# Gates and branch projections with tokens stationary, and another order of pooling, keys and branches, in a two-layer hybrid encoder

## Chip, core and metric

The kernel runs on one core of a Trainium2 chip. A time is the device time of one execution in microseconds (us). The engines are PE (matmul; PEld is its weight load), DVE (VectorE), ACT (ScalarE), POOL (GpSimd) and SP (which issues the weight DMAs).

## What is computed

Two layers of an encoder over 256 tokens of width 1024, all in float32. In each layer three mixers work on one normalised input, each is projected back to 1024, and the three are added under sigmoid gates; then follow an output projection and a gated MLP.

```python
def reference(...):
    for i in range(DEPTH):                                  # 2 layers
        h = _rms_norm(x, norm_mix_pre[i])                   # x: 256 tokens x 1024
        proj = h @ w_in[i]
        u_hy, q, k, v, g_out, gate_lr, u_pool, gate_logits = _split(proj, IN_SPLITS)
        y_hy = _hyena_mixer(u_hy, ...)                      # FFT long convolution, 512 wide
        y_gla = _gla_mixer(q, k, v, g_out, gate_lr, ...)    # gated linear attention, 4 heads
        y_pool = _pool_mixer(u_pool, ...)                   # 4 centred window means less input, 128 x 128 products
        gates = jax.nn.sigmoid(gate_logits).reshape(B, L, N_BRANCHES, D_MODEL)
        merged = (gates[:, :, 0] * (y_hy @ w_br_hyena[i])
                  + gates[:, :, 1] * (y_gla @ w_br_gla[i])
                  + gates[:, :, 2] * (y_pool @ w_br_pool[i]))
        x = x + _rms_norm(merged @ w_out[i], norm_mix_post[i])
        h = _rms_norm(x, norm_ffn_pre[i])
        a, b = _split(h @ ffn_w_up[i], (D_FF, D_FF))        # 2 x 2816
        a = _dwconv3_centred(a, ffn_conv_w[i], ffn_conv_b[i])
        y = (jax.nn.gelu(a, approximate=False) * b) @ ffn_w_down[i]
        x = x + _rms_norm(y, norm_ffn_post[i])
```

## The kernel before

**Matmuls.** Every float32 operand of a large product is split into a high part (ACT copies it with rounding to the matmul's format, L98 through `split` and `split_upper`) and a low part (DVE subtracts, L103), and a product is three matmuls: high by high, high by low, low by high. All matmuls go through `mm` (L112). The normalised input is kept transposed, channels on partitions and 256 tokens along the row (`xt`, four tiles of high and four of low parts in two halves).

**Weights** come in 71 chunks per layer of 128 x 2048 numbers (1 MB), in the order of `order`, by SP into three `raw` buffers (`dma_next`); a chunk's buffer is free when its low half is split off, and then the next chunk is fetched. A split chunk holds four of 37 `big` slots. `unit` writes down one piece of matmul work, forces the splits that it needs, writes down the pending work on its result (`post`), and steps the side work (`tick`: hyena, decay gates, pooling, linear attention), which is written as generators that wait for free slots.

**Two forms of matmul.** With weights stationary (`ftile`, `two_ftiles`) a 128 x 128 block of weights is loaded and 256 tokens stream past it: a chunk is 48 matmuls of 256 columns, and the result lies with channels on partitions. With tokens stationary (`chunk_x_stationary`) a 128 x 128 block of tokens is loaded and 512 columns of weights stream past: a chunk is 24 matmuls of 512 columns, and the result has tokens on partitions. The values, the output projection and the MLP's down projection use the second form; keys, queries, the inputs of hyena and pooling, gates, branches and most of the up projection use the first.

**Order of a layer.** Values and output gate, low-rank decay, hyena inputs, queries, keys (`qk_post(enb, ...)`), pooling inputs (`pool_post`, which starts `pool_pair`: window sums on DVE, then two small products), and then `branch` for hyena, pooling and linear attention: for each half of 512 channels two gate chunks, then one chunk of the branch projection, gate times projection on DVE, and for the later branches the sum. After the third branch the sum is split at once into the operands of the output projection, since it already has channels on partitions. `hyena()` transforms its input, multiplies the spectra on DVE (`p`, `q`, `p2`, `q2`), then asks for the inverse matrices (`ih`, `il`, two DMAs on POOL's queue, L804 and L805), and multiplies by them; its result is the operand of the first branch.

A scheduler sets the final order of instructions on each engine from this text. Around each layer's norms an explicit window keeps the written order. On each engine instructions run in the order that stands in the program.

Of the kernel before, what the change touches and what calls it, by code (L numbers as in the profile page):

```python
# [18 lines left out]
P = 128  # L19
# [11 lines left out]
NCHUNK = 71  # L31


V_HYC = 0
V_FFC = 48
V_GB = 136
V_PS = 148
V_FB = 152
NVEC = 160

UP_ORDER = (0, 4, 1, 5, 2, 6, 3, 7, 8, 9, 10)

# [34 lines left out]
def trunk(ctx: ExitStack, tc: tile.TileContext, a: dict, out: bass.AP):  # L77
# [87 lines left out]
    order = []  # L165
    for i in range(DEPTH):
        base = i * NCHUNK
        order += [("w", base + c) for c in range(4)]
        order.append(("lr", i))
        order += [("w", base + c) for c in range(4, NCHUNK)]  # L170
    pos_of = {o: n for n, o in enumerate(order)}
    raws, wh, wl = {}, {}, {}
    state = {"dma": 0, "h": 0, "l": 0}
# [1 line left out]
    def dma_next(parts=1, between=None):  # L175
        n = state["dma"]
        if n >= len(order):
            return
        kind, c = order[n]
        w = 2048 if kind == "w" else 512  # L180
        r = wpool.tile([P, w], F32, tag="raw", name=f"raw{n}")
        src = a["wts"][c] if kind == "w" else a["lrw"][c]
        for m in range(parts):
            s = slice(m * w // parts, (m + 1) * w // parts)
            nc.sync.dma_start(r[:, s], src[:, s])
            if between is not None and m == 0:
                between()
        raws[n] = r
        state["dma"] = n + 1
# [110 lines left out]
            n += 1  # L300
            assert n < 500, "side work cannot go on"

    pending = deque()
    prog = {"acc": 0.0}

    def unit(chunks, pe, post=None, cost=2.6, free=None):
        for c in chunks:
            while state["l"] < 2 * (c + 1):
                split_half()
        ahead["at"] = min(chunks)  # L310
        pe()
        if free is not None:
            big.put(*wh.pop(free), *wl.pop(free))
        while pending:
            pending.popleft()()
        if post is not None:
            pending.append(post)
        prog["acc"] += cost
        while prog["acc"] >= 2.6 - 1e-6:
            prog["acc"] -= 2.6  # L320
            tick()
            for _ in range(0 if ahead["still"] else 1 if ahead["quiet"] else 2):
                filler()

    def room(shape, dtype=F32):
        n = 0
        while not big.free:
# [239 lines left out]
    def layer(i, xt, chains):  # L567
        base = i * NCHUNK
        cur = {"c": 0}
        nxt = lambda: pos_of[("w", base + cur["c"])]  # L570

        def take():
            n = nxt()
            cur["c"] += 1
            return n
# [149 lines left out]
        def qk_post(dst, pair, scale):  # L725
            def post(ps):
                for z in range(2):
                    d = dst[pair][:, :, z, :]
                    if scale is None:
                        tt(d, ps[:], d, ALU.mult)  # L730
                    else:
                        stt(d, ps[:], scale, d)
            return post

        def hyena():
# [42 lines left out]
                    psm.put(ps)  # L778
            big.put(zth, ztl, even, kf.pop("dft"))
            yh, yl = [], []  # L780
            for b in range(2):
                while len(big.free) < 2:
                    yield
                zr, zi = zz[b][:, 0, :], zz[b][:, 1, :]
                yh.append(big.get([P, 2, DH], F32R))
                yl.append(big.get([P, 2, DH], F32R))
                re, im = kf["k"][b][:, 0, :], kf["k"][b][:, 1, :]
                rm = kf["rm"][:] if b == 0 else re
                p, q = sml.get([P, DH]), sml.get([P, DH])
# [12 lines left out]
            sml.put(kf.pop("rm"))  # L802
            kf["ih"], kf["il"] = big.get([P, 4, L], F32R), big.get([P, 4, L], F32R)
            nc.gpsimd.dma_start(kf["ih"][:], a["ih"])  # L804
            nc.gpsimd.dma_start(kf["il"][:], a["il"])  # L805
            yield
            while handles.get("x0") is None:
                yield
            while len(big.free) < 2:
# [29 lines left out]
        two_ftiles(take(), xt, qk_post(eb, 0, float(P ** -0.5)))  # L839
        handles["x0"] = True  # L840
        two_ftiles(take(), xt, qk_post(eb, 1, float(P ** -0.5)))
        for pair in range(2):
            two_ftiles(take(), xt, qk_post(enb, pair, None))


        pw = sml.get([P, 4, P])
        nc.gpsimd.dma_start(pw[:], a["poolw"][i])
# [5 lines left out]
        def pool_pair(g0, u):  # L853
            if g0 == 0:
                split(pwh[:], pwl[:], pw[:])
            while len(big.free) < 2:
                yield
            a1, a2 = big.get([P, 2, W]), big.get([P, 2, W])
            d = sml.get([P, 2, L])
# [42 lines left out]
        def pool_post(g0):  # L902
            def post(ps):
                u = big.get([P, 2, W])
                nc.gpsimd.memset(u[:, :, 0:PAD], 0.0)
                nc.gpsimd.memset(u[:, :, PAD + L:], 0.0)
                act(u[:, :, PAD:PAD + L], ps[:])
                pool_h.append(start(pool_pair(g0, u)))
            return post

        two_ftiles(take(), xt, pool_post(0))
        two_ftiles(take(), xt, pool_post(2))

        y_gl = {}

# [80 lines left out]
        merged = []  # L996
        mhl = {}

        def branch(b, ready):
            for half in range(2):  # L1000
                gate = room([P, 4, L])
                if b == 0:
                    merged.append(gate)
                for pair in range(2):
                    s = slice(pair * 2, pair * 2 + 2)

                    def post(ps, s=s, gate=gate):
                        act(gate[:, s, :], ps[:], AF.Sigmoid)
                    two_ftiles(take(), xt, post)
                ys = ready()  # L1010
                n = take()
                if b == 2 and half == 1:
                    flush()
                    big.put(*xt[0], *xt[1])
                if b == 2:
                    mhl[half] = big.get([P, 4, L], F32R), big.get([P, 4, L], F32R)
                for pair in range(2):
                    ps = psm.get([P, 2, L])
                    s = slice(pair * 2, pair * 2 + 2)

                    def post(ps=ps, s=s, gate=gate, half=half, pair=pair):
                        tt(gate[:, s, :], gate[:, s, :], ps[:], ALU.mult)
                        psm.put(ps)
                        if b > 0:
                            tt(merged[half][:, s, :], merged[half][:, s, :], gate[:, s, :], ALU.add)
                        if b == 2:
                            split(mhl[half][0][:, s, :], mhl[half][1][:, s, :], merged[half][:, s, :])
                        if pair == 1:
                            if b > 0:
                                big.put(gate)  # L1030
                            if b == 2:
                                big.put(merged[half])

                    def pe(ps=ps, pair=pair):
                        for j in range(2):
                            ftile(n, ([ys[0]], [ys[1]]), pair * 2 + j, ps[:, j, :], width=512, kn=4)
                    unit([n], pe, post, free=n if pair else None)

        def ready_pool():
            drain(*pool_h)  # L1040
# [7 lines left out]
            drain(f_gla)  # L1048
            return y_gl["h"], y_gl["l"]

        branch(0, ready_hy)
        big.put(*handles["y_hy"])
        branch(1, ready_pool)
        big.put(*y_pl)
        ahead.update(chunks=7, reserve=4)
        branch(2, ready_gla)
        big.put(y_gl["h"], y_gl["l"])
# [4 lines left out]
        g_pre2 = gain(i, 2, nc.gpsimd)  # L1062
        xt2 = xt_alloc()
        ns = [take() for _ in range(4)]
        flush()
        mx = ([mhl[0][0], mhl[1][0]], [mhl[0][1], mhl[1][1]])
        ch2 = []
        for t in range(2):
# [3 lines left out]
            for c in range(4):  # L1072
# [5 lines left out]
                if t == 0 and c == 2:  # L1078
                    open_window()
        flush()  # L1080
        big.put(*mx[0], *mx[1])


# [318 lines left out]
```

## Time and profile before

| | |
|---|---|
| median of 3 runs | 902.9 us (901.14 to 904.99) |
| the profiled execution | 900.64 us, of which the span of instructions is 898.9 us |
| PE busy | 886.0 us, 99% of the span |
| DVE busy | 630.9 us, 70% |
| ACT busy | 505.8 us, 56% |

A busy PE is not one at its peak: matmuls are pipelined and overlap in the records, so that the mean duration of one is longer than the distance from one to the next. What one costs is therefore read from a stretch in which nothing else runs, as its length by the number of matmuls.

### The profile page before, as it was taken

The page shows a single profiled execution, that of the slowest core. Times are in us where ns is not written, and L with a number is a line of the kernel's source. Part 1 is how long each engine was busy: PE and PEld are TensorE (multiplying, and loading weights), DVE is VectorE, ACT ScalarE, POOL GpSimd, SP SyncE. Part 2 cuts the span into 40 slices and gives each one's busy share as a digit, 9 for nine tenths or more (in the row PEclk, how much of TensorE's full clock was granted, in tenths as well). Part 3 has the DMA queues.
Part 4 walks back from the last instruction along what each step waited for, and adds up shares of the span by engine and source line. Part 5 has one row for each costly group of instructions (what it writes and reads, how often), then busy time and mean ns, then how long its engine had stood idle before and what let it go on. Part 6 is the DMA issues. An engine that isn't in the chain of part 4 may idle for free.

```text
span 898.9 us, 15183 instructions
## 1 busy us (share of the span) xinstructions
PE 886.0 (99%) x6272; PEld 830.5 (92%) x6272; DVE 630.9 (70%) x910; ACT 505.8 (56%) x797; POOL 35.0 (4%) x80
## 2 busy tenths in 40 slices
PE   8999999999999999999999999999999999999997
PEld 6899998999988999998888999999998899999885
DVE  5899979665667698765288888865854967776612
ACT  6778746544355776545167865664542766554511
POOL 3000000100010000000010000000000000000000
PEclk9999999999999999999999999999999999999999
DMA  8853545546537426555439545263743583555601
GB/s 290 343 198 129 187 145 178 197 169 246 196 116 268 156 95 240 182 188 205 170 104 337 181 141 198 96 236 141 245 177 141 189 301 125 183 188 178 221 1 47
DMA packets 26021, 164.62 MB, mean 183 GB/s; under 512 B 3178, under 2 KB 3317, under 8 KB 8032
## 3 DMA queue, kind: packets, MB, share of 16 engines
q1 hardware_dynamic: 22464, 151.70, 47.3%
q0 software_dynamic: 3488, 11.95, 4.1%
q8 instruction: 49, 0.80, 0.4%
q14 instruction: 20, 0.16, 0.1%
HBM read 162.59 MB, written 1.05 MB: 182 GB/s over the span
## 4 chain that ended last, share of the span: by engine, by line
PE 96%; DMA 2%; DVE 2%; issue 0%; ACT 0%; SPq 0%; DVEq 0%; POOLq 0%; ACTq 0%
PE p L112 94%; DMA b<-in_il 1%; DVE b L103 1%; DMA raw<-in_wts 1%; PE p L356 1%; PE p L1132 0%; DVE b L106 0%; PE p L749 0%; PE p L965 0%; ACT b L98 0%; SPq L151 0%; DVE s L923 0%; DVE x L106 0%; DVEq L1398 0%; ACT s L98 0%
## 5 line engine op out<-in xcount | busy, mean ns | idle before, releaser
L112 PE MATMUL p<-b,b 128*128 128x256 f32 (+2 forms) x5958 | 854.2, 304 | 5.3 <-DVE b L103 3.5
L112 PEld LDWEIGHTS p<-b,b 128*128 128x128 f32 x5958 | 794.4, 191 | 55.2 <-DVE b L103 4.8
L103 DVE TENSOR_TENSOR b<-raw,b 128x1024 fp32r<-128x1024 f32 x286 | 342.5, 1216 | 123.6 <-ACT b L98 71.2
L98 ACT ACTIVATE b<-raw 128x1024 fp32r<-128x1024 f32 x288 | 290.9, 1045 | 189.1 <-PE p L112 146.7
L103 DVE TENSOR_TENSOR b<-p,b 128x512 f32<-128x512 f32 (+2 forms) x64 | 40.5, 651 | 63.4 <-ACT s L98 51.6
L98 ACT ACTIVATE s<-p 128x256 f32<-128x256 f32 (+3 forms) x50 | 20.5, 414 | 77.5 <-PE p L112 77.2
L98 ACT ACTIVATE b<-p 128x512 f32<-128x512 f32 (+3 forms) x78 | 43.5, 566 | 30.2 <-PE p L112 20.3
L106 DVE SCALAR_TENSOR_TENSOR s<-p,vec,s 128x255 f32<-128x255 f32 x104 | 49.3, 478 | 6.4 <-ACT s L98 5.5
L98 ACT ACTIVATE s<-p,vec 128x256 f32<-128x256 f32 x52 | 28.8, 557 | 18.7 <-DVE s L106 15.3
L98 ACT ACTIVATE s<-s 128x512 f32<-128x512 f32 (+6 forms) x52 | 27.7, 532 | 13.4 <-DVE s L106 8.2
L103 DVE TENSOR_TENSOR b<-b,b 128x512 f32<-128x512 f32 (+4 forms) x34 | 26.6, 781 | 8.3 <-ACT b L98 7.9
L98 ACT ACTIVATE b<-s 128x512 fp32r<-128x512 f32 x38 | 23.7, 625 | 13.1 <-DVE s L103 13.0
L98 ACT ACTIVATE b<-b 128x512 fp32r<-128x512 f32 (+3 forms) x22 | 16.3, 742 | 24.8 <-DVE b L103 23.6
L103 DVE TENSOR_TENSOR b<-s,b 128x512 fp32r<-128x512 f32 x38 | 25.9, 684 | 5.2 <-ACT b L98 5.2
L103 DVE TENSOR_TENSOR b<-b,p 128x512 f32<-128x512 f32 x24 | 16.3, 684 | 10.1 <-PE p L112 9.9
L98 ACT ACTIVATE b<-b,s 128x128 f32<-128x128 f32 x64 | 20.5, 391 | 1.0 <-DVE s L674 0.9
L106 DVE SCALAR_TENSOR_TENSOR b<-p,vec,b 128x255 f32<-128x255 f32 (+1 forms) x40 | 19.1, 477 | 2.6 <-ACT b L98 2.5
L103 DVE TENSOR_TENSOR s<-s,p 128x512 f32<-128x512 f32 x22 | 15.0, 684 | 8.4 <-ACT s L98 8.0
L109 DVE TENSOR_SCALAR mse<-ssq 128x1 f32<-128x1 f32 (+1 forms) x24 | 4.7, 196 | 18.7 <-ACT s L98 14.9
L103 DVE TENSOR_TENSOR s<-s,s 128x512 f32<-128x512 f32 (+2 forms) x24 | 15.6, 662 | 2.0 <-ACT s L98 2.0
L369 POOL TENSOR_TENSOR rstd<-mse,mhalf 128x1 f32<-128x1 f32 x16 | 8.9, 554 | 209.1 <-DVE mse L109 209.1
L112 PE MATMUL p<-b,s 128*128 128x128 f32 (+1 forms) x80 | 15.7, 315 | 0.0
(95 smaller groups left out, 289.8 us busy)
## 6 DMA issues: line engine op xcount, KB each, us to landing
raw<-in_wts SPq DMA_DIRECT2D x140, 1024.0 KB, 5.0
b<-in_gains POOLq DMA_DIRECT2D x7, 512.0 KB, 6.0
raw<-in_wts SPq DMA_DIRECT2D x4, 512.0 KB, 7.3
b<-in_dft POOLq DMA_DIRECT2D x4, 512.0 KB, 7.0
x<-in_x SPq DMA_DIRECT2D x4, 256.0 KB, 4.4
b<-in_gw POOLq DMA_DIRECT2D x2, 512.0 KB, 5.8
b<-in_fw POOLq DMA_DIRECT2D x2, 512.0 KB, 6.7
b<-in_decay POOLq DMA_DIRECT2D x2, 512.0 KB, 8.0
```

The source lines that it names most:

```text
L98: ins = nc.scalar.activation(o, i, func, **kw)
L103: nc.vector.tensor_tensor(out=o, in0=x, in1=y, op=op)
L106: nc.vector.scalar_tensor_tensor(out=o, in0=x, scalar=s, in1=y, op0=op0, op1=op1)
L109: nc.vector.tensor_scalar(out=o, in0=x, scalar1=s1, scalar2=s2, op0=op0, op1=op1)
L112: ins = nc.tensor.matmul(o, w, x, start=start, stop=stop).ins
L356: nc.tensor.transpose(ps[k // 4][:, k % 4, :], h[:, k * P:(k + 1) * P], ident[:])
L369: nc.gpsimd.tensor_tensor(out=r[:], in0=e[:], in1=mhalf[:, 0:1], op=ALU.pow)
```

## The change

**Gates and branches** now have tokens stationary. Two gate chunks are fetched as a pair: two DMAs of half a chunk each put columns 0 to 255 of both next to one another, so that a row of 512 weights is contiguous in each raw tile. Each of the two DMAs writes pieces of 1 KB (before, a row of 8 KB). A gate half is then four units of 12 matmuls of 512 columns, two per block of 128 tokens, and a branch projection two such units. Gates, products and sums have tokens on partitions. The output projection needs channels on partitions, so the sum of the three branches is transposed at its end (`merge_up`: four PE transposes of 128 x 128, then the split), once for each half and block of tokens; a list `later` writes this down one unit after the sum.

**Order.** Pooling inputs come before the keys (`CHUNK_ORDER`), and the branches run as pooling, hyena, linear attention. The weights are fetched in that order. `hyena()` asks for the inverse matrices before it multiplies the spectra, and takes them as soon as four slots are free.

```diff
--- before.py
+++ after.py
@@ -31,12 +31,20 @@
+PAIRED = tuple(c for b in range(3) for c in range(16 + 6 * b, 22 + 6 * b) if (c - 16) % 3 < 2)
...
+CHUNK_ORDER = (*range(12), 14, 15, 12, 13, *range(22, 28), *range(16, 22), *range(28, NCHUNK))
...
@@ -180,6 +187,12 @@
         src = a["wts"][c] if kind == "w" else a["lrw"][c]
+        if kind == "w" and c % NCHUNK in PAIRED:
+            side = (c % NCHUNK - 16) % 3
+            for m in range(2):
+                src = a["wts"][c - side + m][:, side * 1024:(side + 1) * 1024].rearrange("p (k c) -> p k c", c=256)
+                nc.sync.dma_start(r[:].rearrange("p (k c) -> p k c", c=512)[:, :, m * 256:(m + 1) * 256], src)
+            parts = 0
...
@@ -311,8 +324,12 @@
+        done = list(later)
+        later.clear()
         while pending:
             pending.popleft()()
+        for f in done:
+            f()
...
@@ -778,8 +795,15 @@
             yh, yl = [], []
+            while len(big.free) < 4:
+                yield
+            kf["ih"], kf["il"] = big.get([P, 4, L], F32R), big.get([P, 4, L], F32R)
+            nc.gpsimd.dma_start(kf["ih"][:], a["ih"])
+            nc.gpsimd.dma_start(kf["il"][:], a["il"])
             for b in range(2):
                 while len(big.free) < 2:
+                    yield
+                while len(sml.free) < 4:
                     yield
...
@@ -800,10 +824,6 @@
             sml.put(kf.pop("rm"))
-            kf["ih"], kf["il"] = big.get([P, 4, L], F32R), big.get([P, 4, L], F32R)
-            nc.gpsimd.dma_start(kf["ih"][:], a["ih"])
-            nc.gpsimd.dma_start(kf["il"][:], a["il"])
-            yield
...
@@ -839,9 +859,6 @@
-        for pair in range(2):
-            two_ftiles(take(), xt, qk_post(enb, pair, None))
...
@@ -910,6 +927,8 @@
         two_ftiles(take(), xt, pool_post(0))
         two_ftiles(take(), xt, pool_post(2))
+        for pair in range(2):
+            two_ftiles(take(), xt, qk_post(enb, pair, None))
...
@@ -996,17 +1015,32 @@
+        def merge_up(half, t):
+
+            ps = psm.get([P, 4, P])
+            for k in range(4):
+                nc.tensor.transpose(ps[:, k, :], merged[half][:, t, k * P:(k + 1) * P], ident[:])
+            s = slice(t * P, (t + 1) * P)
+            split(mhl[half][0][:, :, s], mhl[half][1][:, :, s], ps[:])
...
-                gate = room([P, 4, L])
+                gate = room([P, 2, 512])
...
-                    def post(ps, s=s, gate=gate):
-                        act(gate[:, s, :], ps[:], AF.Sigmoid)
-                    two_ftiles(take(), xt, post)
+                n0, n1 = take(), take()
+                for t in range(2):
+                    ps = psm.get([P, 512])
+
+                    def post(ps=ps, t=t, gate=gate):
+                        act(gate[:, t, :], ps[:], AF.Sigmoid)
+                        psm.put(ps)
+                    for j, nj in enumerate((n0, n1)):
+                        unit([nj, n1 if t else n0], lambda: chunk_x_stationary(nj, xt, t, ps[:], j),
+                             post if j else None, free=nj if t else None)
...
                         if b == 2:
-                            split(mhl[half][0][:, s, :], mhl[half][1][:, s, :], merged[half][:, s, :])
...
+                            later.append(lambda: merge_up(half, t))
...
-                        for j in range(2):
-                            ftile(n, ([ys[0]], [ys[1]]), pair * 2 + j, ps[:, j, :], width=512, kn=4)
...
+                        for k in range(4):
+                            h, l = weights(n, k * 512, 512)
+                            mm(ps[:], ys[0][:, k, s], h, k == 0, False)
+                            mm(ps[:], ys[0][:, k, s], l, False, False)
+                            mm(ps[:], ys[1][:, k, s], h, False, k == 3)
...
@@ -1048,10 +1083,10 @@
-        branch(0, ready_hy)
+        branch(0, ready_pool)
+        big.put(*y_pl)
+        branch(1, ready_hy)
         big.put(*handles["y_hy"])
-        branch(1, ready_pool)
-        big.put(*y_pl)
         ahead.update(chunks=7, reserve=4)
         branch(2, ready_gla)
...
@@ -1062,7 +1097,6 @@
         ns = [take() for _ in range(4)]
-        flush()
```

**The order on PE at the first gates of layer 0.** A row names the output bank (`p`), then the operand that streams past, then the one that is loaded, then the size. `b_1` to `b_4` are the tokens (high parts 1 and 2, low parts 3 and 4), the others are weights. Before:

```order
L112 MATMUL p_49_1522<-b_1_103,b_100_1231 128x256
L112 MATMUL p_49_1522<-b_3_105,b_100_1231 128x256
L112 MATMUL p_49_1522<-b_1_103,b_101_1232 128x256
L112 MATMUL p_49_1522<-b_2_104,b_102_1299 128x256
L112 MATMUL p_49_1522<-b_4_106,b_102_1299 128x256
L112 MATMUL p_49_1522<-b_2_104,b_103_1300 128x256
```

And now:

```order
L120 MATMUL p_50_1505<-b_105_1323,b_1_103 128x512
L120 MATMUL p_50_1505<-b_106_1324,b_1_103 128x512
L120 MATMUL p_50_1505<-b_105_1323,b_3_105 128x512
L120 MATMUL p_50_1505<-b_107_1327,b_2_104 128x512
L120 MATMUL p_50_1505<-b_108_1328,b_2_104 128x512
L120 MATMUL p_50_1505<-b_107_1327,b_4_106 128x512
```

The operands have changed places and the columns have doubled. In the whole program 4736 matmuls of 256 columns become 3008, 1152 of 512 become 2016, and 32 transposes (L1022) are new.

**PE at the first branch projection of layer 0.** Before, `p_51` is a product of pooling, `p_55` one of linear attention, and `p_54` and `p_57` are the hyena branch, whose operand (`b_121`, `b_122`) is hyena's result:

```order
L112 MATMUL p_51_1579<-s_34_1456,s_24_1312 128x256
L112 MATMUL p_52_1652<-b_2_104,b_109_1362 128x256
L112 MATMUL p_55_1754<-b_47_434,b_49_436 128x128 x4
L112 MATMUL p_54_1724<-b_121_1488,b_110_1365 128x256
L112 MATMUL p_57_1772<-b_121_1488,b_110_1365 128x256
L112 MATMUL p_54_1724<-b_122_1489,b_110_1365 128x256
L112 MATMUL p_54_1724<-b_121_1488,b_111_1366 128x256
```

Now `p_53` and `p_55` are the pooling branch (`b_114`, `b_115` is pooling's result), and `p_52` and `p_54` are hyena's inverse transform (`b_110` and `b_111` are the inverse matrices):

```order
L120 MATMUL p_53_1636<-b_118_1429,b_114_1407 128x512
L120 MATMUL p_53_1636<-b_119_1430,b_114_1407 128x512
L120 MATMUL p_53_1636<-b_118_1429,b_115_1408 128x512
L120 MATMUL p_55_1678<-b_118_1429,b_114_1407 128x512
L120 MATMUL p_55_1678<-b_119_1430,b_114_1407 128x512
L120 MATMUL p_55_1678<-b_118_1429,b_115_1408 128x512
L120 MATMUL p_52_1607<-b_110_1368,b_125_1536 128x256
L120 MATMUL p_52_1607<-b_111_1369,b_125_1536 128x256
L120 MATMUL p_54_1653<-b_110_1368,b_125_1536 128x256
L120 MATMUL p_54_1653<-b_111_1369,b_125_1536 128x256
```

The first branch no longer takes hyena's result; the inverse transform now stands among the matmuls of the pooling branch and of the next gates.

**POOL's queue in layer 0.** Before (L804, L805 are the inverse matrices, L860 a memset in pooling, L905 and L906 the padding of its input):

```order
L847 DMA s_22_1309<-in_poolw 128x512
L522 MEMSET b_73_840 1x512
L804 DMA b_115_1440<-in_ih 128x1024
L860 MEMSET b_117_1446 128x2
L805 DMA b_116_1441<-in_il 128x1024
L905 MEMSET b_114_1436 128x2x8
```

And now:

```order
L864 DMA s_22_1166<-in_poolw 128x512
L877 MEMSET b_103_1280 128x2
L539 MEMSET b_73_840 1x512
L922 MEMSET b_102_1268 128x2x8
L923 MEMSET b_102_1268 128x2x8
L801 DMA b_110_1368<-in_ih 128x1024
L922 MEMSET b_109_1359 128x2x8
L923 MEMSET b_109_1359 128x2x8
L802 DMA b_111_1369<-in_il 128x1024
```

The two fetches now stand behind the padding of the first and of the second pooling input. The first waits for the slot of weights whose last matmul is number 638 of PE's order, the second for one whose last matmul is number 650; before, these were numbers 688 and 700. Up to about number 640 PE's two orders hold the same count of matmuls of the same shapes.

## Rows read from the trace of the kernel before

**Rows 1.** The page of the profile, parts 1 and 2: the span, and of each engine the busy time, its share of the span and its instructions; then the TensorE clock that was granted, in tenths, over 40 equal slices.
```profile
span 898.9 us, 15183 instructions
...
PE 886.0 (99%) x6272; PEld 830.5 (92%) x6272; DVE 630.9 (70%) x910; ACT 505.8 (56%) x797; POOL 35.0 (4%) x80
...
PEclk9999999999999999999999999999999999999999
```

**Rows 2.** The page, part 4: the chain of work that ended last, its shares by engine.
```profile
PE 96%; DMA 2%; DVE 2%; issue 0%; ACT 0%; SPq 0%; DVEq 0%; POOLq 0%; ACTq 0%
```

**Rows 3.** All that the matmul engine waited for in the whole span: us in total, times, longest.
```profile
PE p L112 <- DVE b L103: 3.5, 3, 2.2
PE p L112 <- ACT b L98: 1.4, 1, 1.4
PE p L112 <- DVE rmask L246: 1.2, 1, 1.2
PE p L112 <- DMA b<-in_il: 0.5, 1, 0.5
```

**Rows 4.** Groups of instructions with the shapes kept apart (count | busy us, mean ns of one | idle before), in the stretch 200 to 240 us alone, which lies in the gates and branch projections of layer 0.
```profile
L112 PE MATMUL p<-b,b 128*128 128x256 f32 x335 | 40.4, 283 | 0.0
```

**Rows 5.** The timeline of PE from 420 to 440 us, in the down projection of layer 0 (start, us, engine, line, names, shapes, count).
```profile
419.83 20.34 PE L112 MATMUL p<-b,b 128*128 128x512 f32 x89
```

**Rows 6.** The chain in order of time (start, us, what), where matmuls of 512 columns and transposes follow one another: the output projection of layer 0 with the transposes of the pre-norm (L356), and the transposes of the channel-mixing part (L1132).
```profile
261.89 0.87 PE p L356 x8
262.77 10.91 PE p L112 x48
...
294.76 0.44 PE p L1132 x4
...
316.53 0.59 PE p L1132 x4
```

**Rows 7.** The chain again, in layer 0 where it leaves the matmul engine.
```profile
113.49 9.00 DMA b<-in_il
122.49 0.04 issue
122.54 13.96 PE p L112 x114
...
143.21 0.61 DVE b L103
143.82 0.04 issue
143.86 20.52 PE p L112 x170
```

**Rows 8.** The timeline of the stretch 96 to 150 us, all engines (start, us, engine, line, operation, names, shapes, count, and in brackets the idle time before and who ended it). b<-raw,b of 128x1024 on DVE is the low half of a weight split; L804 and L805 fetch the inverse matrices.
```profile
100.59 1.22 DVE L103 TENSOR_TENSOR b<-raw,b 128x1024 fp32r<-128x1024 f32 x1
...
107.30 2.47 DVE L103 TENSOR_TENSOR b<-p,b 128x512 f32<-128x512 f32 x4
...
110.89 2.35 DVE L103 TENSOR_TENSOR b<-raw,b 128x1024 fp32r<-128x1024 f32 x2
...
112.06 0.53 POOL L804 DMA_DIRECT2D b<-in_ih  x1 [23.89 <-PE p L112]
...
113.49 0.53 POOL L805 DMA_DIRECT2D b<-in_il  x1 [0.79 <-PE p L112]
...
122.54 14.42 PE L112 MATMUL p<-b,b 128*128 128x256 f32 x118 [0.47 <-DMA b<-in_il]
...
128.55 0.75 DVE L106 SCALAR_TENSOR_TENSOR s<-b,b 128x256 f32<-128x256 f32 x2
...
143.86 6.37 PE L112 MATMUL p<-b,b 128*128 128x256 f32 x51 [2.16 <-DVE b L103]
```

**Rows 9.** Busy time of each engine in stretches of 10 and 20 us (in brackets the count), granted clock, mean share of the DMA engines (1.00 and above is rounding), GB/s.
```profile
90.00:100.00 10.00, 10.00 (x84) 9.96 (x83) 9.38 (x17) 7.57 (x16) 0.00 (x0) 1.00 0.28 89
100.00:110.00 10.00, 10.00 (x75) 9.52 (x75) 9.74 (x18) 7.64 (x16) 0.00 (x0) 1.00 0.86 313
...
130.00:140.00 10.00, 10.00 (x86) 10.00 (x86) 6.95 (x12) 5.71 (x9) 0.64 (x2) 1.00 0.06 7
140.00:150.00 10.00, 7.84 (x67) 7.64 (x66) 10.00 (x19) 6.78 (x12) 0.00 (x0) 1.00 0.58 186
...
200.00:220.00 20.00, 20.00 (x169) 20.00 (x169) 12.55 (x14) 9.52 (x11) 0.00 (x0) 1.00 0.71 263
220.00:240.00 20.00, 20.00 (x169) 20.00 (x168) 12.05 (x14) 9.62 (x12) 1.11 (x2) 1.00 0.48 172
```

**Rows 10.** The page, part 3 (DMA queue: packets, MB, share of the time of 16 engines) and part 6 (DMA issues: KB each, median us to landing).
```profile
q1 hardware_dynamic: 22464, 151.70, 47.3%
q0 software_dynamic: 3488, 11.95, 4.1%
...
raw<-in_wts SPq DMA_DIRECT2D x140, 1024.0 KB, 5.0
```

More of the change, by code (lines that the diff above doesn't have):

```diff
@@ L167, in trunk @@
         base = i * NCHUNK
-        order += [("w", base + c) for c in range(4)]
-        order.append(("lr", i))
-        order += [("w", base + c) for c in range(4, NCHUNK)]
+        order += [("w", base + c) for c in CHUNK_ORDER]
+        order.insert(len(order) - NCHUNK + 4, ("lr", i))
     pos_of = {o: n for n, o in enumerate(order)}
@@ L301, in drain @@
             assert n < 500, "side work cannot go on"
-    pending = deque()
+    pending, later = deque(), []
     prog = {"acc": 0.0}
@@ L569, in layer @@
         cur = {"c": 0}
-        nxt = lambda: pos_of[("w", base + cur["c"])]
+        nxt = lambda: pos_of[("w", base + CHUNK_ORDER[cur["c"]])]
         def take():
@@ L855, in pool_pair @@
                 split(pwh[:], pwl[:], pw[:])
-            while len(big.free) < 2:
+            while len(big.free) < 2 or len(sml.free) < 3:
                 yield
@@ L997, in layer @@
         mhl = {}
+        def merge_up(half, t):
[5 more added lines that the diff above has]
+            psm.put(ps)
+            if t == 1:
+                big.put(merged[half])
         def branch(b, ready):
             for half in range(2):
-                gate = room([P, 4, L])
+                gate = room([P, 2, 512])
                 if b == 0:
                     merged.append(gate)
-                for pair in range(2):
-                    s = slice(pair * 2, pair * 2 + 2)
-                    def post(ps, s=s, gate=gate):
-                        act(gate[:, s, :], ps[:], AF.Sigmoid)
-                    two_ftiles(take(), xt, post)
+                n0, n1 = take(), take()
[3 more added lines that the diff above has]
+                        act(gate[:, t, :], ps[:], AF.Sigmoid)
+                        psm.put(ps)
+                    for j, nj in enumerate((n0, n1)):
+                        unit([nj, n1 if t else n0], lambda: chunk_x_stationary(nj, xt, t, ps[:], j),
+                             post if j else None, free=nj if t else None)
                 ys = ready()
@@ L1016, in branch, with post, pe @@
                     mhl[half] = big.get([P, 4, L], F32R), big.get([P, 4, L], F32R)
[L1017 to L1022, printed above, removed]
+                for t in range(2):
+                    ps = psm.get([P, 512])
+                    def post(ps=ps, gate=gate, half=half, t=t):
+                        g, m = gate[:, t, :], merged[half][:, t, :]
+                        tt(g, g, ps[:], ALU.mult)
                         psm.put(ps)
                         if b > 0:
-                            tt(merged[half][:, s, :], merged[half][:, s, :], gate[:, s, :], ALU.add)
+                            tt(m, m, g, ALU.add)
+                            if t == 1:
+                                big.put(gate)
                         if b == 2:
-                            split(mhl[half][0][:, s, :], mhl[half][1][:, s, :], merged[half][:, s, :])
[L1028 to L1034, printed above, removed]
-                        for j in range(2):
-                            ftile(n, ([ys[0]], [ys[1]]), pair * 2 + j, ps[:, j, :], width=512, kn=4)
-                    unit([n], pe, post, free=n if pair else None)
+                            later.append(lambda: merge_up(half, t))
+                    def pe(ps=ps, t=t):
+                        s = slice(t * P, (t + 1) * P)
+                        for k in range(4):
[3 more added lines that the diff above has]
+                            mm(ps[:], ys[1][:, k, s], h, False, k == 3)
+                    unit([n], pe, post, free=n if t else None)
         def ready_pool():
@@ L1080, in layer @@
         flush()
+        assert not later
         big.put(*mx[0], *mx[1])
```

## The prediction

> **What bounds the kernel now.** The page's first lines come first [rows 1]: PE is busy for 886.0 of 898.9 us, at the full granted clock (2.4 GHz) all along. The chain that ended last agrees: 96% of it is PE [rows 2]. A busy PE can hide stalls, so the list of its waits comes next [rows 3]: they add up to 6.6 us in the whole span, and the longest is 2.2 us. So the time is the number of matmuls times what one costs, plus a few us. What one costs is the view that matters, with shapes kept apart and read from stretches of one shape only [rows 4, 5]. Between 200 and 240 us 335 matmuls of 256 columns make 40.4 us; the last one's pipelined tail (mean duration 283 ns less the distance to the next, some 0.16 us) is to be taken off: (40.4 - 0.16) / 335 = 120.1 ns each. Between 420 and 440 us 89 matmuls of 512 columns make 20.34 us: (20.34 - 0.16) / 89 = 226.7 ns. The chain gives a second reading for 512: 48 in 10.91 us, 227.3 ns [rows 6]. Two matmuls of 256 thus cost 240.2 ns and one of 512 that does the same work 226.7 to 227.3: every matmul carries some 13 ns besides its columns.
>
> Last, the two places where the chain leaves PE [rows 7], both in layer 0. At 122.54 PE waits 0.47 us for the DMA of the second inverse matrix, whose issue stood on POOL until 113.49 [rows 8]. At 143.86 it waits 2.16 us for DVE, which writes the low half of hyena's result, the operand of the first branch [rows 8]. DVE is nearly full around there: 9.4 to 10.0 of 10 us in three of the four stretches [rows 9].
>
> **The matmuls.** Per layer 12 gate chunks and 6 branch chunks change form, in two layers 36 chunks with 48 matmuls each: 1728 of 256 columns go and 864 of 512 come (the counts of the program say the same). Gain: 864 x (240.2 - 226.7) = 11.7 us, with 227.3 for the new form 11.1; I take 11.4. The new form is the one that values, output and down projection have now, so its price is measured on operands of the same type and size, with a new stationary block for each matmul, as here. All of it lies on the chain, since PE is never idle there [rows 4].
>
> On this the Trainium skill speaks against the change ("TensorE: Matmul & The Clock Gate", section Back-to-back issue gap): it gives a warm gap of N / 2.4 + 2.5 ns. An estimate from that page would be 864 x 2.5 = 2.2 us of gain, and the whole sum would then come out at 902 us. The trace's 13 ns decides; the page's 215.8 ns for 512 columns is also 11 ns under the row.
>
> **The transposes.** 32 are new, in 8 groups of four (2 layers, 2 halves, 2 blocks of tokens). Groups of four of that shape take 0.44 us on the chain, one 0.59 [rows 6]; eight take 0.87, so 0.11 each. 8 x 0.44 = 3.5 us to 8 x 0.59 = 4.7; I take 4.0, since a group also delays the matmul behind it a little. They are on the chain for their whole length. Their splits (ACT, then DVE, 0.6 us each by the 512-column pitch of [rows 8]) replace those of the sum, one for one. What they could add is a wait: the output projection needs the last ones. The order puts 18 matmuls of 512 columns, 4.1 us, between the last branch matmul and the last but one group, and six more with a group until the first matmul that reads the result. The two DVE steps and the split take about 2.5 us. I cost it at nothing; without that cover it would be 2 to 3 us per layer.
>
> **The two stalls.** The fetches of the inverse matrices were released at 112.06 and 113.49 [rows 8] by PE's matmuls 688 and 700; now they need 638 and 650. Fifty matmuls at 0.12 us make 6 us: they go out at about 106 and 107.5 and, with the 9 us of [rows 7], land by 117. The memsets that stand ahead of them on POOL take a tenth of a us, and wait for slots that PE has left by then. Their first reader is now past matmul 800, so this 0.5 us is gone.
>
> The 2.2 us go if pooling's result is in time, which is now the first branch's operand. PE: matmul 638 is at about 112 - 6 = 106 us; then come 102 matmuls of 256 columns and 36 of 512, 12.2 + 8.2 us, until the product of the second pooling input at 126.3 us. DVE: the weight split that stands at 100.59 [rows 8] comes no later now (two multiplications of keys ahead of it are gone). From it to the low half of the second pooling input 36 instructions stand in the order: 5 of 1024 columns at a pitch of 1.13 us, 18 of about 512 at 0.60, 8 of about 256 at 0.34 and 5 small ones [rows 8], 19.8 us, so about 121.6. That is 4.7 us early. Then 39 matmuls of 512 and some of 256 columns, 9.7 us, stand before the one that reads pooling's last but one low part; DVE has 5.7 us of work for it after the release of its slots at 126.3. Again some 4 us are left. Hyena's result, now wanted only two halves (32 us) later, has all the time. So I credit both, 0.5 + 2.2 = 2.6 us by the rows' own digits (0.47 + 2.16), with bounds of 0 (the wait is only passed on) and 2.6. In layer 1 PE waited for nothing there and has nothing to gain.
>
> **What is left at nothing.** ACT and DVE have the same splits, sigmoids and products of the same sizes. In the gates DVE is busy 12.5 of 20 us [rows 9], and a faster PE asks for weights 5% sooner: still covered. SP issues 24 more DMAs, which its queue has room for: a chunk of 1 MB lands 5.0 us after its issue [rows 10] and PE uses one in 24 x 0.227 = 5.4 us, with three buffers. Smaller pieces are the one thing that the trace does not show (third rival).
>
> **Sum.** -11.4 + 4.0 - 2.6 = -10.0 us against the profiled execution (898.9 us span, 900.6 us), so 890.6 there; that run lies 2.3 us under the median of 902.9. Against the median: **892.9 us**.
>
> **Rivals.** First, *the stall moves*. With DVE as full as [rows 9] shows it, the first branch waits for pooling as it did for hyena, or an ACT step ahead of DVE is late. Against it speak the 4 us of room worked out above; for it, that each of those sums assumes that DVE waits for nothing. Then the 2.6 us stay (-7.4, 895.5), or up to 3 us are added to them (898.5).
>
> Second, *the 13 ns don't come*: the distance between shapes belongs to the stages, not to the form. Then the transposes are paid for nothing, 4.0 - 2.6 = +1.4 us, 904.3. Against it: both stretches have PE busy to the last digit and no wait, at the same clock [rows 1, 4, 5]. The rule of the Trainium skill named above would come out near here, and the rows bear it out no better.
>
> Third, the one that ends on the other side: *the paired fetch starves PE*. A gate chunk is now 1024 pieces of 1 KB, over 16 engines 64 each. The two queues' rows give 0.473 x 16 x 898.9 / 22464 = 303 ns for a mean packet of 6.75 KB and 0.041 x 16 x 898.9 / 3488 = 169 ns for one of 3.43 KB [rows 10]. A line through them gives about 72 ns for 1 KB, 4.6 us per chunk. A half needs two such chunks and a plain one (2.9 us by the same line), 12.1 us, against 72 x 0.227 = 16.3 us of PE. It decides from (16.3 - 2.9) / 2 = 6.7 us per chunk, 105 ns a piece; at 111 ns the 12 halves have eaten the 10 us, and at 169 ns (as if size didn't count) it is 24.5 - 16.3 = 8.2 us a half, some 990 us. The line puts it far off; the row that it is nearest to is 4.6 us.
>
> That the change does not do what it says is excluded for the forms and the fetches by the order; for the time it is the first rival.
>
> **How the numbers follow.** The forecast (891 to 895) has 0.66. The stall moved, 895 to 898.4: 0.16; the same with something added, up to 902: 0.07. No gain from the form, 904: 0.03. The fetch starves PE, above 905: 0.08, part of it lightly. Less time than 889.5 would need more than all terms at their best. The range 889.5 to 900 leaves out the last two cases and part of the third. About 0.5%, 4.5 us, is what a measurement of this kernel tells from no change, so faster ends at 898.4 and slower begins at 907.4: faster 0.82, same 0.10, slower 0.08.
>
> **What would show it.** In the profile after: matmuls of 256 and 512 columns at 120 and 227 ns in stretches of one shape; eight groups of four transposes of 0.44 to 0.6 us; no wait of PE for the inverse matrices and none over 0.5 us between 110 and 160 us; PE's own total about 10 us less. A list of PE's waits with DVE at the first pooling branch would mean the first rival; with the raw weights' DMA, or ACT waiting for it for more than the page shows now in the gates, the third; a new form at 240 ns, the second. The forecast is wrong if PE's waits grow above 10 us in all.

## The result, and the profile after

The changed kernel takes 892.07 us (median, 890.94 to 892.75), the kernel before 902.02 beside it: ratio 0.988, 95% interval 0.9861 to 0.9899. The forecast was 892.9. Its profiled execution has a span of 889.8 us, 9.1 less than before [rows 1].

The page after, parts 1 and 4 (busy us, share of the span, instructions; then the chain by engine), and below it all waits of PE:

```profile
span 889.8 us, 13575 instructions
...
PE 878.9 (99%) x5440; PEld 788.3 (89%) x5440; DVE 630.3 (71%) x910; ACT 504.3 (57%) x797; POOL 35.1 (4%) x80
...
PE 97%; DVE 1%; DMA 1%; ACT 0%; issue 0%; SPq 0%; DVEq 0%; POOLq 0%; ACTq 0%
```

```profile
PE p L120 <- ACT b L106: 1.6, 1, 1.6
PE p L120 <- DVE rmask L259: 1.2, 1, 1.2
PE p L120 <- DVE b L111: 1.1, 1, 1.1
```

PE is still the bound and lost 7.1 us of busy time; DVE and ACT are within 1.5 us of what they were. The waits fell from 6.6 to 3.9 us: the one for the inverse matrix is gone, and so is the longest one for DVE [rows 3].

Shapes kept apart, whole span (count | busy us, mean ns of one | idle before), then the gates alone from 205 to 220 us:

```profile
L120 PE MATMUL p<-b,b 128*128 128x512 f32 x2016 | 475.6, 392 | 2.9 <-ACT b L106 1.6 <-DVE b L111 1.1
L120 PE MATMUL p<-b,b 128*128 128x256 f32 x3008 | 372.0, 283 | 0.0
```

```profile
L120 PE MATMUL p<-b,b 128*128 128x512 f32 x68 | 15.6, 389 | 0.0
```

In the gates the new form costs (15.6 - 0.16) / 68 = 227.1 ns, as in the down projection before [rows 5]. Over the whole span a pair of 256 costs 2 x 372.0 / 3008 = 247.3 ns and one of 512 costs 475.6 / 2016 = 235.9: 11.4 ns apart.

The chain in order of time, from the hyena transform to the output projection of layer 0 (start, us, what):

```profile
96.30 73.31 PE p L120 x451
...
221.60 0.44 PE p L1022 x4
222.04 2.31 PE p L120 x10
224.35 0.44 PE p L1022 x4
224.79 14.99 PE p L120 x66
239.78 0.44 PE p L1022 x4
240.22 0.94 PE p L120 x4
241.16 0.44 PE p L1022 x4
241.59 14.10 PE p L120 x62
```

From 96 to 170 us the chain does not leave PE, where it left it twice before [rows 7]. The four groups of transposes are on it, 0.44 us each, with no wait around them. POOL's timeline shows the fetches, at 106.10 and 107.67 instead of 112.06 and 113.49 [rows 8]:

```profile
106.10 0.53 POOL L801 DMA_DIRECT2D b<-in_ih  x1 [6.34 <-PE p L120]
...
107.67 0.53 POOL L802 DMA_DIRECT2D b<-in_il  x1 [0.33 <-DVE s L111]
```

### The profile page after: what moved, and what is told of

Read it like the earlier page. It is cut to its first block, busy times and chain, and to the rows that moved or that the text cites. A ratio compares the mean times of both kernels' runs of the same rounds, so it can differ in the third digit from the quotient of the medians.

```text
span 889.8 us, 13575 instructions
## 1 busy us (share of the span) xinstructions
PE 878.9 (99%) x5440; PEld 788.3 (89%) x5440; DVE 630.3 (71%) x910; ACT 504.3 (57%) x797; POOL 35.1 (4%) x80
## 4 chain that ended last, share of the span: by engine, by line
PE 97%; DVE 1%; DMA 1%; ACT 0%; issue 0%; SPq 0%; DVEq 0%; POOLq 0%; ACTq 0%
PE p L120 96%; DMA raw<-in_wts 1%; PE p L373 1%; PE p L1167 0%; PE p L1022 0%; DVE b L114 0%; DVE b L111 0%; PE p L766 0%; PE p L984 0%; ACT b L106 0%; SPq L159 0%; DVE x L114 0%; DVEq L1433 0%; ACT s L106 0%; POOLq L1433 0%
## 5 line engine op out<-in xcount | busy, mean ns | idle before, releaser
L120 PE MATMUL p<-b,b 128*128 128x256 f32 (+2 forms) x5094 | 845.6, 326 | 2.9 <-ACT b L106 1.6
L120 PEld LDWEIGHTS p<-b,b 128*128 128x128 f32 x5094 | 746.6, 190 | 85.3 <-DVE b L111 2.5
L111 DVE TENSOR_TENSOR b<-p,b 128x512 f32<-128x512 f32 (+2 forms) x72 | 46.1, 657 | 69.2 <-ACT s L106 44.6
L106 ACT ACTIVATE b<-p 128x512 f32<-128x512 f32 (+3 forms) x86 | 47.7, 568 | 57.4 <-PE p L120 32.6
L111 DVE TENSOR_TENSOR b<-b,b 128x512 f32<-128x512 f32 (+4 forms) x26 | 21.1, 812 | 2.5 <-ACT b L106 2.0
L106 ACT ACTIVATE b<-b 128x1024 fp32r<-128x1024 f32 (+3 forms) x14 | 11.3, 806 | 9.4 <-DVE b L111 8.3
```

Of the source, the lines that this page charges most:

```text
L120: ins = nc.tensor.matmul(o, w, x, start=start, stop=stop).ins
```

## The experiments

Ratios are to the kernel before, run beside each experiment on the same chip, with their 95% intervals. Medians of different sessions compare to about 1 us.

The runs of one kernel spread with TensorE's granted clock. The kernel before takes 900.0 to 900.8 us in the eleven runs on record whose mean granted clock is 0.999, and 904.2 to 904.7 in the three at 0.993. The traces show where the clock falls. From 10 to 20 us (stretch, its length, then busy us and counts of PE, PEld, DVE, ACT and POOL, then the granted clock, DMA share and GB/s), in the kernel before (0.999 over the whole span) and in e4 below (0.994):

```profile
10.00:20.00 10.00, 8.69 (x39) 6.11 (x38) 8.80 (x21) 8.65 (x22) 5.69 (x11) 1.00 0.96 315
```

```profile
10.00:20.00 10.00, 9.29 (x31) 6.77 (x32) 6.88 (x18) 7.20 (x20) 5.69 (x11) 0.67 0.97 317
```

A mean of 0.67 is two thirds of the stretch at the lower level (1.2 GHz). Runs of one and the same kernel meet either, so a second comparison is given below, of runs at 0.999 alone: the kernel before has a median of 900.3 us there (11 runs), the changed kernel 891.2 (2 runs), 9.0 us less.

**e1_halved: the number of matmuls alone.** Each matmul of 512 columns in gates and branches became two of 256:

```diff
+    def chunk_x_halved(n, xt, t, ps, half):
...
+            for c in (slice(0, 256), slice(256, 512)):
...
+                mm(ps[:, c], xth[:, k, s], h[:, c], first, False)
+                mm(ps[:, c], xth[:, k, s], l[:, c], False, False)
+                mm(ps[:, c], xtl[:, k, s], h[:, c], False, last)
```

> The changed kernel with one thing altered: in the gates and branch projections every matmul of 512 columns is written as two of 256, with the same tokens loaded for each half. Orientation, order, fetches and transposes stay; 864 matmuls come back, as many as the kernel before had. My theory (each matmul carries 13 ns besides its columns, whichever operand is loaded): +864 x 13.4 = +11.6 us on the changed kernel, so about 903.6 against 902.0 of the kernel before, ratio 1.002. Rival (it is the orientation, tokens loaded and weights streaming, that is cheaper): no change from the changed kernel, ratio 0.988.

Measured: 901.38 us, ratio 1.000 (0.9989 to 1.001), 9.3 us above the changed kernel by the medians, 9.9 by the spans (899.7), 10.0 by the runs at 0.999 (901.3), 10.8 by the ratios. The matmul groups of its profile are those of the kernel before again:

```profile
L120 PE MATMUL p<-b,b 128*128 128x256 f32 x4736 | 584.5, 284 | 0.0
L120 PE MATMUL p<-b,b 128*128 128x512 f32 x1152 | 271.5, 392 | 3.0 <-ACT b L106 1.8 <-DVE b L111 1.2
```

So the gain is the number of matmuls: 9.3 to 10.8 us for 864, 11 to 12 ns each. Which operand is loaded makes no difference beyond about 1 us: e1 loads tokens and takes as long as the kernel before, and the transposes and the waits, which also differ between the two, nearly cancel. What the runs cannot part is a matmul from the weight load that comes with it. Every matmul has its own in all these kernels (PE and PEld both count 5440 instructions in the changed kernel, 6304 in e1).

**e5_double_tr and e6_no_tr: the transposes.** One writes each transpose of the sum twice (`for k in (0, 1, 2, 3, 0, 1, 2, 3)`), one leaves them out:

> The changed kernel with every transpose of the sum written twice into the same place: 32 transposes more. My theory (they lie on PE's chain for their whole length, 0.11 us each, and the switch is not paid twice): +3.5 us on the changed kernel, 895.6, ratio 0.992. Rival (they fill time in which PE would wait for the splits or the sums, so they cost nothing): ratio 0.988.

> The changed kernel without the transposes of the sum: the sum is split where it lies, so the output projection multiplies numbers in the wrong places and the output is not the reference's; all else is the same. My theory (3.5 to 4.7 us on the chain, 4.0 taken): -4.0 us on the changed kernel, 888.1, ratio 0.984. Rival (the output projection would wait for the splits anyway): less than 1 us of it, ratio 0.987.

Measured: 895.91 us, ratio 0.9926 (0.9909 to 0.9943), and 886.85 us, ratio 0.9833 (0.9813 to 0.9853): +3.8 and -5.2 us by the medians, +4.1 and -4.2 by the ratios, +2.7 and -4.7 by the few runs at 0.999. In the chain of the first, a group of four is now one of eight, and takes twice the time:

```profile
222.74 0.88 PE p L1022 x8
```

**The order and the fetch, each alone, with either form.** Six kernels fill the table of three switches: form (weights or tokens stationary), order (pooling inputs and pooling branch first, or not), and fetch (inverse matrices ahead of the spectra, or behind).

```diff
+            while len(big.free) < 4:
+                yield
+            kf["ih"], kf["il"] = big.get([P, 4, L], F32R), big.get([P, 4, L], F32R)
+            nc.gpsimd.dma_start(kf["ih"][:], a["ih"])
+            nc.gpsimd.dma_start(kf["il"][:], a["il"])
             for b in range(2):
                 while len(big.free) < 2:
+                    yield
+                while len(sml.free) < 4:
                     yield
...
-        branch(0, ready_hy)
+        branch(0, ready_pool)
+        big.put(*y_pl)
+        branch(1, ready_hy)
         big.put(*handles["y_hy"])
-        branch(1, ready_pool)
-        big.put(*y_pl)
```

The first part is the fetch, the second the branches' part of the order. The wait for four free `sml` slots is in every kernel of the table but the kernel before.

> The kernel before with the new order alone: pooling inputs ahead of keys, branches as pooling, hyena, attention, inverse matrices fetched ahead of the spectra. Gates and branches keep weights stationary, no transposes of the sum. My theory (the order is worth the two waits of layer 0, 2.6 us): 899.4, ratio 0.997, and no wait of PE over 0.5 us between 110 and 160 us. Rival (the waits only move, or went because the forms changed): ratio 1.000 with a wait in that stretch.

> The changed kernel with the old order: keys ahead of pooling inputs, branches as hyena, pooling, attention, inverse matrices fetched after the spectra; tokens stationary in gates and branches, with the transposes. My theory: the forms are worth -11.4 + 4.0 = -7.4 us and the two waits stay at about 2.6 us: 894.6, ratio 0.992. Rival (with faster gates the first branch asks for hyena's result sooner, so the waits grow, by up to the 1.6 us that PE gains in 3 chunks): 896, ratio 0.994. Second rival (the order was worth nothing): ratio 0.988.

> The kernel before with the earlier fetch of the inverse matrices alone. My theory: the wait of 0.5 us for the fetch goes, the wait for DVE after it (2.2 us) stays or takes part of the 0.5 us back, since DVE writes hyena's result behind other work: 0 to -0.5 us, ratio 0.9995 to 1.000. Rival (the late matrices are what makes DVE late, so both waits go): -2.6 us, ratio 0.997.

> The changed kernel with the inverse matrices asked for after the spectra, as before; forms and order as changed. Theory after the first runs (the early fetch alone removes both waits of layer 0, and so does the order alone, since the first branch then reads pooling's result; one of the two is enough): no change, ratio 0.988. Rival (the early fetch is what counts, the order does nothing): the waits come back, +3.8 us, ratio 0.992.

> The kernel before with the new order of pooling, keys and branches, and with the late fetch: gates and branches with weights stationary. Theory (one of the two is enough): -3.8 us as with the fetch alone and with both, ratio 0.996. Rival (the order does nothing for the waits): ratio 1.000, with PE waiting over 1 us for DVE or the matrices between 110 and 165 us.

> The changed kernel with the old order (keys ahead of pooling, hyena the first branch) and the early fetch: tokens stationary. Theory (one of the two is enough): as the changed kernel, ratio 0.988. Rival (with the faster gates the first branch asks for hyena's result too soon, so the order is needed as well): a wait of 1 us or more at the first branch, ratio 0.990 to 0.992.

| ratio (interval), median us | weights stationary | tokens stationary |
|---|---|---|
| old order, late fetch | before: 1, 901.8 to 902.6 | e3: 0.9916 (0.9898 to 0.9934), 894.1 |
| old order, early fetch | e4: 0.9958 (0.9944 to 0.9971), 898.2 | e11: 0.9898 (0.9881 to 0.9915), 893.9 |
| new order, late fetch | e10: 0.9952 (0.9935 to 0.9968), 897.3 | e9: 0.9885 (0.9867 to 0.9904), 892.9 |
| new order, early fetch | e2: 0.9958 (0.9944 to 0.9972), 897.9 | changed: 0.988 (0.9861 to 0.9899), 892.1 |

With weights stationary, the fetch alone, the order alone and both give the same, 0.4 to 0.5% (at 0.999 e2, e4 and e10 take 897.3, 896.9 and 897.0 us, 3.0 to 3.4 less than the kernel before). PE waits nowhere over 0.2 us between 110 and 165 us in any of the three. One rival is untested: all three edits hold the wait for free `sml` slots too, and no kernel has that wait alone with weights stationary. With tokens stationary e3 has it alone, and a wait of PE stays.

My theory for e4 fell: the earlier fetch does not just remove the 0.5 us, the wait for DVE goes as well. PE's timeline of e4 has no gap from 99.81 us on:

```profile
99.81 35.67 PE L112 MATMUL p<-b,b 128*128 128x256 f32 x285
135.31 0.88 PE L112 MATMUL p<-s,s 128*128 128x256 f32 x6
136.03 9.81 PE L112 MATMUL p<-b,b 128*128 128x256 f32 x81
145.68 0.61 PE L112 MATMUL p<-s 128*128 128x128 f32 x4
```

Two things moved. The first is PE's order. With the matrices there sooner, the scheduler puts the last matmul of the inverse transform at number 853 instead of 879, and 59 gate matmuls (7.1 us at 0.12) between it and the matmuls that read the last quarter of hyena's result; before there was one.

The second is DVE, but this shows only when the two traces are laid side by side at the same instruction. e4's trace has the fall of the clock at its start, and its weight split of [rows 8] begins at 102.95 us instead of 100.59: up to where the kernel before waits for the matrices, e4 is 2.36 us late.

```profile
102.95 1.22 DVE L103 TENSOR_TENSOR b<-raw,b 128x1024 fp32r<-128x1024 f32 x1
```

DVE's multiplication of the transform's second half, and its last low half of hyena's result, in the kernel before and then in e4:

```profile
137.23 0.68 DVE L103 TENSOR_TENSOR b<-p,b 128x512 f32<-128x512 f32 x1
...
143.13 0.68 DVE L103 TENSOR_TENSOR b<-b,b 128x512 fp32r<-128x512 f32 x1
```

```profile
135.79 0.68 DVE L103 TENSOR_TENSOR b<-p,b 128x512 f32<-128x512 f32 x1
...
142.83 0.69 DVE L103 TENSOR_TENSOR b<-b,b 128x512 fp32r<-128x512 f32 x1
```

Less the 2.36 us, the multiplication is 3.8 us earlier and the low half 2.7 us. PE, for its part, reaches the first matmul that reads this low half 2.0 us later: by the count of the order at 146.04 us, against 141.70 before, where the wait of 2.16 us began. Either of the two is about enough for 2.16 us, and no run parts them. So the rival that I had named, that the late matrices are what makes DVE late, is borne out at least in part.

With tokens stationary and neither of the two (e3), PE waits 1.40 us in the same stretch, but for another DVE instruction: the product of gate and projection, which ends just before, and not the low half of hyena's result. PE's wait, and that product:

```profile
146.47 8.27 PE L120 MATMUL p<-b,b 128*128 128x512 f32 x35 [1.40 <-DVE b L111]
```

```profile
145.73 0.68 DVE L111 TENSOR_TENSOR b<-b,p 128x512 f32<-128x512 f32 x1
```

e11 and e9 lie 1.8 and 0.8 us above the changed kernel by the medians, with overlapping intervals; at 0.999 they take 891.7 and 890.8 us against 891.2. So the second of the two adds nothing that these runs can show. e9 shows a wait of 0.29 us for the matrices, e11 one of 0.23 us for DVE.

**e7_host_pairs and e8_pieces128: the fetch in small pieces.** e7 lays the paired weights out in memory as they are read, one DMA per chunk with rows of 8 KB. e8 interleaves the pair in pieces of 128 B:

```diff
-                src = a["wts"][c - side + m][:, side * 1024:(side + 1) * 1024].rearrange("p (k c) -> p k c", c=256)
-                nc.sync.dma_start(r[:].rearrange("p (k c) -> p k c", c=512)[:, :, m * 256:(m + 1) * 256], src)
+                src = a["wts"][c - side + m][:, side * 1024:(side + 1) * 1024].rearrange("p (k c) -> p k c", c=32)
+                nc.sync.dma_start(r[:].rearrange("p (k m c) -> p k m c", m=2, c=32)[:, :, m, :], src)
```

> The changed kernel with the gate weights laid out in memory in the order in which they are read, so that each gate chunk is one DMA with rows of 8 KB, as the other chunks; the same numbers in the same places on the chip. My theory (the smaller pieces are hidden behind PE): 0, ratio 0.988. Rival (the pieces of 1 KB slow the fetch or the neighbours of the fetch): up to -2 us, ratio 0.986.

> The changed kernel with the two gate chunks of a pair interleaved in pieces of 128 B instead of 1 KB, eight times as many pieces; columns of the gates come out in another order than those of the branches, so the output is not the reference's. My theory (a half decides at 6.7 us per gate chunk): the 1 KB pieces add 0.014 of 16 engines' time for some 21900 packets more in the changed kernel, 46 ns each, near a price by bytes. With a price by bytes and 9 ns a piece (fit of the same records) 128 B cost 14 ns, 8192 pieces over 16 engines 7 us per chunk: at the edge, a loss of 0 to 10 us. If the price of a piece does not fall below some 30 ns, 15 us per chunk and some 190 us lost.

Measured: 890.62 us, ratio 0.987 (0.9852 to 0.9887), and 890.81 us, ratio 0.9872 (0.9847 to 0.9897). Neither can be told from the changed kernel (e8 has two runs); the loss of 0 to 10 us that I had put at the edge for e8 did not come. The weight queue (packets, MB, share of the time of 16 engines) and the landing of a paired half chunk (KB, median us), of the changed kernel and then of e8:

```profile
q1 hardware_dynamic: 44352, 151.70, 48.7%
...
raw<-in_wts SPq DMA_DIRECT2D x52, 512.0 KB, 5.3
```

```profile
q1 hardware_dynamic: 216384, 151.70, 57.4%
...
raw<-in_wts SPq DMA_DIRECT2D x52, 512.0 KB, 6.9
```

For the same bytes 172032 more packets took (0.574 x 889.3 - 0.487 x 889.8) x 16 = 1230 us of one DMA engine, 7 ns each. PE's waits in e8 add up to 3.6 us (3.9 in the changed kernel), and none is for a DMA.

**e12_nb2: the same form where transposes are not shared.** In the up projection the changed kernel, like the one before, has 4 chunks with tokens stationary, each with four transposes of its own; here 2 (`NB = 2`, and the layout of the weights to match).

> The changed kernel with two chunks less per layer in that form: in the up projection 2 instead of 4 chunks of the ungated half have tokens stationary. There each chunk pays for its own four transposes, where gates and branches share 16 among 18 chunks. Theory (prices of the runs so far): 4 groups of four transposes go, -4 x 0.5 = -2.0 us, 96 matmuls of 512 columns become 192 of 256, +96 x 11.7 ns = +1.1 us: -0.9 us, ratio 0.987. Rival (those chunks are the cover for the norm of the second block of tokens: with two, 5.4 us of matmuls instead of 10.9, PE waits for it): +2 to +6 us per layer, ratio 0.993 or more.

Measured: 900.31 us, ratio 0.9985 (0.9973 to 0.9998), 8.2 us above the changed kernel. The rival was right: all waits of PE in e12 add up to 10.1 us, against 3.9 in the changed kernel. PE's timeline around the transposes of the pre-norm (L373) in layer 0:

```profile
255.93 8.42 PE L120 MATMUL p<-b,b 128*128 128x512 f32 x36
266.19 1.23 PE L373 MATMUL p<-ident,b 128*128 128x128 f32 x8 [1.84 <-DVE b L114]
268.44 0.96 PE L120 MATMUL p<-b,b 128*128 128x512 f32 x4 [1.03 <-ACT b L106]
...
270.76 8.05 PE L120 MATMUL p<-b,b 128*128 128x512 f32 x45 [0.90 <-DVE b L111]
```

With 36 matmuls instead of 48 between the two groups, PE waits three times, 3.8 us by these rows. Those chunks pay as cover for the norm of the second block of tokens, whatever their transposes cost.

## Why the prediction was right

The sum was right to a microsecond, and its terms to within 2 us. That it came within 0.1 us by the medians (-10.0 forecast, -9.95 measured) is luck: the runs of one kernel lie up to 4.7 us apart, and at the same clock the change is -9.0.

**Matmuls, -11.4 us: the mechanism right, the size at the upper end.** e1 gives 9.3 to 10.8 us, by the way of comparing. The price came from stretches of one shape, and there it holds (227.1 ns in the gates). By the whole-span groups after the change, first matmuls of a group and those behind transposes or small products included, a pair is 11.4 ns dearer than one of 512, 864 x 11.4 = 9.8 us; what takes the difference is not shown. The rule of the Trainium skill ("TensorE: Matmul & The Clock Gate", Back-to-back issue gap), 2.5 ns besides the columns, agrees no better after than before: e1's price is more than four times that. The page gives that rule for an isolated matmul and says that in a stream of weight loads and matmuls both set the spacing; this kernel is such a stream, so the prediction's estimate used it where that section does not.

**Transposes, +4.0 us: confirmed** from both sides, +2.7 to +4.1 when doubled and -4.2 to -5.2 when left out. They are on the chain for their whole length and the output projection waits for none of them, as the order promised.

**The two waits, -2.6 us: gone, worth slightly more, and not only for the reason given.** e2, e4 and e10 put them at 3.6 to 5.3 us by the medians, at 3.0 to 3.4 at the same clock. What failed is the condition "the 2.2 us go if pooling's result is in time, which is now the first branch's operand". With the new order the waits go (e10), but they go without it as well: e4 keeps hyena as the first branch and has no wait. I had costed the fetch at 0.5 us because the chain's second departure named DVE; the earlier matrices let PE end the inverse transform sooner, so DVE had its input sooner, and they let the scheduler put other work on PE ahead of the reader. The walk through PE's and DVE's orders held in its outcome: the fetches went out at 106.10 and 107.67 (106 and 107.5 forecast), and pooling's second product started at 128.19 (126.3 forecast) with no wait.

**One sign was misstated.** "PE's own total about 10 us less" does not follow from the sum: waits are not busy time, so the terms give -11.4 + 4.0 = -7.4 us, and 7.1 was measured. The other signs came as written.

**The rivals.** In the changed kernel the stall did not move; without the order and the early fetch (e3) a wait of 1.4 us for another DVE instruction stands in its stretch. The form did bring its gain. The paired fetch starved nothing, and its price was misjudged in the safe direction: the line through two queues has 31 ns a packet besides the bytes (of its 72 ns for 1 KB). By the change of the queue's share from before [rows 10], (0.487 x 889.8 - 0.473 x 898.9) x 16 = 130 us for 21888 more packets, it is 6 ns; against e7, whose queue has a share of 47.0% of 889.5 us with as few packets as before, 11 ns. Even with pieces of 128 B PE's waits did not grow.

In all: -10.0 + 3.7 - 3.2 = -9.5 us by the middle of the experiments at the same clock, -9.0 measured there. No version with the right output is clearly faster than the changed kernel.

## What to carry to other kernels

When PE is busy all along, count matmuls as well as columns: here the form with the longer stream wins about 11 ns per matmul saved, and pays if the transposes that the new layout needs are shared (16 for the 18 chunks of a layer; by these prices a chunk saves 864 / 36 = 24 matmuls, 0.26 us, less than four transposes of its own, 0.44 us). When a wait names an engine, ask what that engine waited for, and what stands just ahead of the waiting instruction: here an earlier fetch made the engine earlier and put independent matmuls there, both at once. Before start times of two traces are compared, look for an instruction that both have and take off its difference; here 2.36 us of another clock at the start hid that DVE was earlier. Before removing dear work, look whether it covers something.

## What was not expected

A weight fetch in pieces of 128 B instead of 8 KB rows cost no time in the kernel: some 7 ns per packet, and a landing of 6.9 us for half a chunk, where pieces of 1 KB took 5.3. And the spread between runs of one kernel goes with TensorE's granted clock: in e4's trace it falls within the first 20 us, and what follows is 2.36 us late.
